# A product-key expert layer on one core: gates of the first half of the tokens are spread while the second half's top-k is still going on

## The chip, the cores and the metric

One core of a Trainium2 chip runs the whole program. The metric is the time of one execution in device microseconds (us); lower is better. All tensors are float32, and products of matrices are made from two parts of each operand (a high part rounded to a format that TensorE takes in one pass, and the low rest): three matmuls, high x high, high x low and low x high, stand for one.

## The reference, cut to what matters

The program is one layer block (modulation, attention, a recurrence, an expert layer) followed by a second one of two layers. The change lies in the expert layer, 256 tokens, width 1024, 16384 experts of one neuron each:

```python
def peer_ffn(h, w_query, sub_keys1, sub_keys2, expert_u, expert_v):
    q = (x @ w_query).reshape(T, 8, 256)
    s1 = einsum('thd,nd->thn', q[..., :128], sub_keys1)      # 128 keys
    s2 = einsum('thd,nd->thn', q[..., 128:], sub_keys2)
    v1, i1 = top_k(s1, 16)
    v2, i2 = top_k(s2, 16)
    cand = (v1[..., :, None] + v2[..., None, :]).reshape(T, 8, 256)
    top_s, top_p = top_k(cand, 16)
    e_idx = i1[top_p // 16] * 128 + i2[top_p % 16]
    gate = softmax(top_s, axis=-1)
    act = gelu(einsum('cd,ced->ce', x, expert_u[e_idx]))
    y = einsum('ce,ced->cd', gate * act, expert_v[e_idx])
```

## The kernel before, in words

The kernel gathers nothing. `peer` (L1026) goes over all 16384 experts in NB = 128 blocks of 128 (block j holds the experts whose first key is j). A first pass computes gelu(x u) for every expert and all 256 tokens and multiplies it by a gate that is 0 for the experts that a token did not choose; a second pass multiplies the result by v. The products of gate and gelu stay in SBUF: G0 holds blocks 0 to 71 (NA = 72), G1 blocks 72 to 127, each block 128 experts x 256 tokens.

*First pass.* `fetch` (L1180) loads one block of u as four transfers from SP's queue into a raw tile `u` (three buffers). `prepare(j)` (L1191) fetches block j+2, transposes block j on DVE (`uT`, three buffers), and makes its high part `uh` on ACT and its low part `ul` on POOL, two halves of 512 columns each (four buffers of either). `products(j)` (L1203) does 24 matmuls of 256 columns on PE, the gelu on ACT, then `prepare(j + 4)`, and then calls `advance`, which gives the side work its share of the block.

*Side work.* A list of generators is worked off by `advance` (L1248): a block brings `pace` units, each yield of a generator costs some. `topk` (L1089) is one head for one half (tile t of 128 tokens) of the tokens: two searches among 128 keys (1.2 units each), one among 256 candidates (1.4), and the lookup of the indices (1), nearly all on DVE; POOL does one multiplication of the lookup (`oh`), and DVE adds it up one step later (`looked_up`). `gates(t)` (L1120) makes the softmax of a half and transposes indices and gates into `pick`. `spread` (L1142) makes the dense gates, four tokens (N = 4) at a step: DVE writes two masks `one0` and `one1` by comparing a row of numbers with the indices, ACT scales `one1` by the gate (four activations), PE multiplies the two into a PSUM tile of 4 x 128 x 128, and this is brought into G: columns of blocks that are already finished are multiplied on DVE (`G<-G,g`), those that are not are copied by ACT (`G<-g`). The masks of a step are made one step ahead. A block that comes later than some gates multiplies its gelu by them in `products` (DVE, `G<-y,G`, where y is the gelu in PSUM). One spread tile takes one of four PSUM banks tagged g, as a block's product does.

Before the change the order of the side work is: the heads of tile 0, two heads of tile 1, `gates(0)`, the other heads of tile 1, `gates(1)`, and only then `spread` over all 256 tokens; its masks lie where the top-k tiles were. Pace is 1.3 during top-k and 1 after.

V, A and P are engines behind `Ordered` (L993), which keeps their instructions in the order in which the program writes them; they all show line L1001. In the trace L106 to L108 are the three matmuls of a product, L1162 the matmul of a spread step, L1312 to L1314 the second pass, L1188 the transfer of u.

The second pass (`second`, L1226) loads v into the raw tiles of `u` and `uT`, five blocks ahead, and makes its high and low parts in `uh` and `ul`.

Of the kernel before, what the change touches and what calls it, by code (L numbers as in the profile page):

```python
# [11 lines left out]
F = mybir.dt.float32  # L12
FR = mybir.dt.float32r
# [7 lines left out]
T = 256  # L21
# [1004 lines left out]
def peer(k, then):  # L1026


    nc, a, tc = k.nc, k.a, k.tc
    mod = k.mod  # L1030
    uu, vv = a["peer_u"][0], a["peer_v"][0]
    NB, NA = 128, 72
    V, A, P = (Ordered(tc, e) for e in (nc.vector, nc.scalar, nc.gpsimd))
    with ExitStack() as es:

# [15 lines left out]
        e2 = ExitStack()  # L1051
# [87 lines left out]
        state = dict(done=0, built=0)  # L1139
        N = 4  # L1140

        def spread(pool, first):  # L1142


            i128 = k.psum([128, 128], tag="o", bufs=2)
            V.tensor_copy(i128, i128s)

            def ones(t0):
                b, g = (pool.tile([128, N, 128], F, name=f"one{i}", bufs=2) for i in range(2))
                for o, i in ((b, 0), (g, 1)):  # L1150
                    V.tensor_tensor(o, i128[:, None, :].to_broadcast([128, N, 128]),
                                    pick[:, i, t0:t0 + N, None].to_broadcast([128, N, 128]), op=OP.is_equal)
                for t in range(N):
                    A.activation(g[:, t], g[:, t], AF.Copy, scale=pick[:, 2, t0 + t:t0 + t + 1])
                return b, g
            nxt = ones(0)
            yield 1
            for t0 in range(0, T, N):
                b, g = nxt
                p = k.psum([128, N, 128])  # L1160
                for t in range(N):
                    nc.tensor.matmul(p[:, t], g[:, t], b[:, t], start=True, stop=True)  # L1162
                if t0 + N < T:
                    nxt = ones(t0 + N)
                n = state["done"]
                for x, at in ((G[0], 0), (G[1], NA)):
                    x, y = x[:, :, t0:t0 + N], p.rearrange("p t j -> p j t")
                    to = at + x.shape[1]
                    c = min(max(n, at), to)
                    if c > at:  # L1170
                        V.tensor_tensor(x[:, :c - at], x[:, :c - at], y[:, at:c], op=OP.mult)
                    if c < to:
                        A.activation(x[:, c - at:], y[:, c:to], AF.Copy)
                state["built"] = t0 + N
                yield (NB - 5 - first) * N / T

        us = {}
        gap(k, pool, GAPS["u"])

        def fetch(j):  # L1180
            if j < NB:
                us[j] = pool.tile([128, 1024], F, name="u", bufs=3)
            elif j < 2 * NB:
                us[j] = pool.tile([128, 1024], F, name=("u", "uT")[j // 3 % 2], bufs=3)
                nc.sync.dma_start(us[j], vv[(j - NB) * 128:(j - NB) * 128 + 128])
            if j < NB:
                for x in range(4):
                    nc.sync.dma_start(us[j][32 * x:32 * x + 32].rearrange("p (g d) -> p g d", g=4),  # L1188
                                      uu[j * 128:j * 128 + 128, 256 * x:256 * x + 256].rearrange("(g p) d -> p g d", g=4))
# [12 lines left out]

        def products(j):  # L1203

            p = k.psum([128, T])
            h, l = (x.rearrange("p (c e) -> p c e", c=8) for x in us.pop(j))
            for c in range(8):
                k.mm3(p, h[:, c], l[:, c], ph[:, c], pl[:, c], c == 0, c == 7)
            n = state["built"]
            o = G[j // NA][:, j % NA]  # L1210
            if n:
                g = k.psum([128, T], tag="y", bufs=2)
                A.activation(g[:, :n], p[:, :n], AF.Gelu)
            if n < T:
                A.activation(o[:, n:], p[:, n:], AF.Gelu)
            if j + 4 < NB:
                prepare(j + 4)
            elif j + 4 == NB:
                for x in range(2, 5):
                    fetch(NB + x)  # L1220
            if n:
                V.tensor_mul(o[:, :n], g[:, :n], o[:, :n])
            state["done"] = j + 1
            advance(pace)

        def second(i):  # L1226

            r = us[NB + i]
            vh, vl = (pool.tile([128, 1024], FR, name=x, bufs=4) for x in ("uh", "ul"))
# [12 lines left out]
        best = [[], []]  # L1242
        side = []
# [27 lines left out]
        for _ in proj_t_steps(k, a["peer_w_query"][0], hh, hl, 0, 2048, use):  # L1271
            step += 1
            for x in best[0]:
                side.append(x)
            best[0].clear()
            advance(1.05)
            if 6 <= step < 22:
                for d, o in turns[:2]:
                    A.activation(d, o.bitcast(F), AF.Copy)
                del turns[:2]  # L1280
            elif step == 25:
                fetch(0)
                fetch(1)
# [837 lines left out]
```

## Time and profile before

| | us |
|---|---|
| three executions | 2318.8, 2332.5, 2334.44 (median 2332.5) |
| the profiled execution | 2320.28 |
| its span in the profile | 2318.2 |
| first pass over u in it | from 487.16 to 926.70 |

The profiled execution is near the fastest of the three. Rows of a timeline give the start, the duration, the engine, the line, the operation and the shape, xN for N instructions that follow each other, and in brackets how long the engine stood idle before and what released it. Instructions of one engine overlap by some hundredths of a microsecond, so the time from start to start is a little less than the duration.

### The profile page before, as it was taken

To read this page: it belongs to the slowest core of one execution; us is meant where nothing else is said; L and a number is where in the kernel's file an instruction comes from. 1 tells how busy PE (TensorE), PEld (TensorE's weight loads), DVE (VectorE), ACT (ScalarE), POOL (GpSimd) and SP (SyncE) were. 2 spreads that over 40 slices of the span, in tenths; PEclk is the share of its full clock that TensorE was granted. 3 is DMA by queue.
4 is the path that set the end of the run, shared out by engine and by line. 5 is a ranking of instruction groups with operands and counts; after the bars stand their busy time and mean duration, and the time that the engine had idled before them with its cause. 6 is when DMAs were issued, how large, how long until landed. Compare 5 with 4: busy or idle time off the path is not lost.

```text
span 2318.2 us, 46849 instructions
## 1 busy us (share of the span) xinstructions
PE 2191.8 (95%) x17962; PEld 2079.0 (90%) x17962; DVE 1735.9 (75%) x3278; ACT 1264.6 (55%) x2689; POOL 809.6 (35%) x811
## 2 busy tenths in 40 slices
PE   6999898789899999999999999899999999989998
PEld 3878587789799999999999999878899999979998
DVE  6888886899877888777776765678875666777664
ACT  3543532735477776555554644447556666536543
POOL 1132320569877777444444100101432221131000
PEclk8999898899999999999999999999999999989999
DMA  7422123447655666666665675323565555516663
GB/s 266 149 92 86 61 73 96 119 107 173 162 148 155 154 150 177 196 196 195 193 193 165 185 219 193 122 74 111 155 202 166 181 162 191 178 36 192 190 200 119
DMA packets 304064, 358.38 MB, mean 155 GB/s; under 512 B 24188, under 2 KB 276576, under 8 KB 302816
## 3 DMA queue, kind: packets, MB, share of 16 engines
q1 hardware_dynamic: 291456, 349.53, 50.0%
q10 hardware_dynamic: 12384, 5.86, 1.0%
q8 instruction: 141, 2.31, 0.4%
q14 instruction: 83, 0.68, 0.1%
HBM read 354.28 MB, written 1.05 MB: 153 GB/s over the span
## 4 chain that ended last, share of the span: by engine, by line
PE 76%; DVE 13%; DMA 3%; ACT 3%; issue 2%; POOL 2%; SPq 0%; ACTq 0%; DVEq 0%; POOLq 0%
PE g L106 12%; PE g L108 12%; PE g L107 12%; PE o L106 4%; PE o L107 4%; PE o L108 3%; PE g L1162 2%; PE y L1314 2%; PE o L1314 2%; PE y L1312 2%; PE o L1312 2%; PE o L1313 2%; PE y L1313 2%; DVE uT L1001 2%; DVE wl L100 2%
## 5 line engine op out<-in xcount | busy, mean ns | idle before, releaser
L99 ACT ACTIVATE wh<-raw 128x1024 fp32r<-128x1024 f32 (+3 forms) x397 | 387.1, 977 | 389.2 <-PE g L107 185.5
L100 DVE TENSOR_TENSOR wl<-raw,wh 128x1024 fp32r<-128x1024 f32 (+3 forms) x381 | 431.6, 1135 | 223.2 <-ACT wh L99 209.8
L106 PE MATMUL g<-xh,wh 128*128 128x256 f32 x1864 | 529.9, 285 | 8.7 <-ACT xh L374 5.8
L108 PE MATMUL g<-xh,wl 128*128 128x256 f32 x1864 | 525.4, 282 | 8.4 <-DVE wl L100 8.3
L107 PE MATMUL g<-xl,wh 128*128 128x256 f32 x1864 | 524.6, 282 | 4.1 <-DVE xl L375 2.7
L1001 POOL TENSOR_TENSOR ul<-uT,uh 128x512 fp32r<-128x512 f32 x320 | 411.6, 1306 | 188.4 <-ACT uh L1001 188.4
L106 PEld LDWEIGHTS g<-xh,wh 128*128 128x128 f32 x1864 | 357.5, 192 | 15.2 <-ACT xh L374 6.9
L108 PEld LDWEIGHTS g<-xh,wl 128*128 128x128 f32 x1864 | 356.2, 191 | 12.1 <-DVE wl L100 11.7
L107 PEld LDWEIGHTS g<-xl,wh 128*128 128x128 f32 x1864 | 356.4, 191 | 6.1 <-DVE xl L375 3.5
L1001 ACT ACTIVATE uh<-uT 128x512 fp32r<-128x512 f32 x384 | 221.3, 627 | 146.5 <-POOL ul L1001 76.5
L108 PE MATMUL g<-ph,ul 128*128 128x256 f32 x1024 | 291.1, 284 | 7.7 <-POOL ul L1001 7.6
L106 PE MATMUL g<-ph,uh 128*128 128x256 f32 x1024 | 292.8, 286 | 3.7 <-ACT uh L1001 2.0
L107 PE MATMUL g<-pl,uh 128*128 128x256 f32 x1024 | 289.1, 282 | 0.0
L108 PEld LDWEIGHTS g<-ph,ul 128*128 128x128 f32 x1024 | 194.7, 190 | 11.3 <-POOL ul L1001 11.1
L106 PE MATMUL o<-hh,wh 128*128 128x256 f32 x704 | 197.8, 281 | 1.6 <-DVE t L1374 1.6
L106 PEld LDWEIGHTS g<-ph,uh 128*128 128x128 f32 x1024 | 195.1, 191 | 4.6 <-ACT uh L1001 2.3
L107 PE MATMUL o<-hl,wh 128*128 128x256 f32 x704 | 197.4, 280 | 0.0
L108 PE MATMUL o<-hh,wl 128*128 128x256 f32 x704 | 197.1, 280 | 0.0
L107 PEld LDWEIGHTS g<-pl,uh 128*128 128x128 f32 x1024 | 195.3, 191 | 0.0
L1001 DVE TENSOR_TENSOR al<-G,ah 128x256 fp32r<-128x256 f32 x128 | 173.9, 1359 | 17.2
L154 POOL TENSOR_TENSOR sql<-sq,sqh 128x256 fp32r<-128x256 f32 x48 | 48.8, 1018 | 340.1 <-ACT sqh L153 336.0
L1001 DVE STREAM_TRANSPOSE uT<-u 128x1024 f32<-128x1024 f32 x128 | 157.8, 1235 | 2.3 <-DMA u<-in_peer_u_dram 1.9
(772 smaller groups left out, 5456.4 us busy)
## 6 DMA issues: line engine op xcount, KB each, us to landing
u<-in_peer_u_dram SPq DMA_DIRECT2D x512, 128.0 KB, 2.6
raw<-in_ffn_w_gate_dram SPq DMA_DIRECT2D x44, 1024.0 KB, 5.6
raw<-in_ffn_w_up_dram SPq DMA_DIRECT2D x44, 1024.0 KB, 5.3
u<-in_peer_v_dram SPq DMA_DIRECT2D x64, 512.0 KB, 4.3
uT<-in_peer_v_dram SPq DMA_DIRECT2D x64, 512.0 KB, 4.2
raw<-in_ffn_w_down_dram SPq DMA_DIRECT2D x32, 1024.0 KB, 5.1
raw<-in_ada_w_dram SPq DMA_DIRECT2D x24, 1024.0 KB, 5.2
raw<-in_w_in_dram SPq DMA_DIRECT2D x13, 1024.0 KB, 5.7
```

Of the source, the lines that this page charges most:

```text
L99: nc.scalar.activation(h, v, AF.Copy)
L100: self.sub.tensor_tensor(l, v, h.bitcast(F), op=OP.subtract)
L106: nc.tensor.matmul(out, sh, mh, start=first, stop=False)
L107: nc.tensor.matmul(out, sh, ml, start=False, stop=False)
L108: nc.tensor.matmul(out, sl, mh, start=False, stop=last)
L154: self.sub.tensor_tensor(l, sq, h.bitcast(F), op=OP.subtract)
L1001: return lambda *args, **kw: self.tc.keep_in_program_order(f(*args, **kw))
L1162: nc.tensor.matmul(p[:, t], g[:, t], b[:, t], start=True, stop=True)
L1312: nc.tensor.matmul(o, vh[:, s], ah, start=i == 0 and c % 2 == 0, stop=False, skip_group_check=True)
L1313: nc.tensor.matmul(o, vh[:, s], al, start=False, stop=False, skip_group_check=True)
L1314: nc.tensor.matmul(o, vl[:, s], ah, start=False, stop=i == NB - 1, skip_group_check=True)
```

## The change

Spreading the gates of tile 0 begins as soon as these exist, and runs between the pieces of tile 1's top-k (`both` takes from either generator in proportion 48 to 42 units); tile 1 is spread afterwards. So that tile 1's scores, which lie in G0, are not overwritten, blocks are worked in another order: 72 to 127 first (G1), then 0 to 71 (G0). The masks get tiles of their own beside the top-k tiles, and for that room the raw tile `u` has two buffers instead of three and `ul` three instead of four; u is fetched one block ahead, v four. Pace is 0.95, then 1.2 once `both` begins, then 1.

```diff
+    blocks = [*range(NA, NB), *range(NA)]
...
-        def spread(pool, first):
+        def spread(t, new, first=None):
...
             def ones(t0):
-                b, g = (pool.tile([128, N, 128], F, name=f"one{i}", bufs=2) for i in range(2))
+                b, g = (new(i, t0 // N % 2) for i in range(2))
...
-            nxt = ones(0)
-            yield 1
-            for t0 in range(0, T, N):
+            last = 128 * t + 128
+            nxt = ones(128 * t)
+            yield 1.5
+            for t0 in range(128 * t, last, N):
...
-                n = state["done"]
-                for x, at in ((G[0], 0), (G[1], NA)):
+                for x, at, n in ((G[0], 0, max(state["done"] - NB + NA, 0)), (G[1], NA, NA + state["done"])):
                     x, y = x[:, :, t0:t0 + N], p.rearrange("p t j -> p j t")
                     to = at + x.shape[1]
                     c = min(max(n, at), to)
                     if c > at:
                         V.tensor_tensor(x[:, :c - at], x[:, :c - at], y[:, at:c], op=OP.mult)
                     if c < to:
                         A.activation(x[:, c - at:], y[:, c:to], AF.Copy)
                 state["built"] = t0 + N
-                yield (NB - 5 - first) * N / T
+                yield 1.25 if first is None else (NB - 5 - first) * N / 128
...
-                us[j] = pool.tile([128, 1024], F, name="u", bufs=3)
+                us[j] = pool.tile([128, 1024], F, name="u", bufs=2)
...
-            fetch(j + 2)
+            fetch(j + 1)
             uT = pool.tile([128, 1024], F, name="uT", bufs=3)
-            h, l = (pool.tile([128, 1024], FR, name=x, bufs=4) for x in ("uh", "ul"))
+            h, l = (pool.tile([128, 1024], FR, name=x, bufs=n) for x, n in (("uh", 4), ("ul", 3)))
...
-            o = G[j // NA][:, j % NA]
+            o = G[blocks[j] // NA][:, blocks[j] % NA]
...
-            if i + 5 < NB:
-                fetch(NB + i + 5)
+            if i + 4 < NB:
+                fetch(NB + i + 4)
...
-        side += best[0] + best[1][:2] + [gates(0)] + best[1][2:] + [gates(1)]
+        ow = e2.enter_context(tc.tile_pool(reuse_waits="tile", name="po", bufs=1, side="right"))
+        new = lambda i, turn: ow.tile([128, N, 128], F, name=f"one{i}", bufs=2)
+        side += best[0] + [both(chain(gates(0), spread(0, new)), chain(*best[1], gates(1)), 48, 42)]
...
-        pace = 1.3
+        pace = 0.95
         for j in range(NB):
-            if not side and not state["built"]:
-                e2.close()
-                ow = e2.enter_context(tc.tile_pool(reuse_waits="tile", name="po", bufs=1, side="right"))
-                side.append(spread(ow, j))
+            if not side and state["built"] == 128:
+                assert blocks[j] < 46
+                side.append(spread(1, new, j))
                 pace = 1
```

In the built program PE's spread steps stand behind blocks 43 to 122 before, and behind 17 to 77 and 82 to 123 now.

DVE, one spread step late in the first pass of the kernel before, when G0 (G_4181) is finished and G1 (G_5114) in part; `one` are masks, `g` the spread tile, `y` a gelu in PSUM; what an instruction waits for stands in brackets:

```order
L1001 TENSOR_TENSOR G_5114<-y_10256,G_5114 128x180 [waits Activation_49]
L1001 TENSOR_TENSOR one_10278<-o_7192,pick 128x512 [waits DVE_49]
L1001 TENSOR_TENSOR one_10279<-o_7192,pick 128x512 [waits DVE_49]
L1001 TENSOR_TENSOR G_4181<-G_4181,g_10273 128x72x4 [waits PE_49]
L1001 TENSOR_TENSOR G_5114<-G_5114,g_10273 128x28x4 [waits Activation_49]
L1001 STREAM_TRANSPOSE uT<-u 128x1024 [waits DMAHW6_49,DMAHW1_49,DMAHW7_49,DMAHW0_49,Pool_49]
```

The first spread step with a finished block in the changed kernel, on DVE, where G1 is G_5109, with the pieces of top-k around it:

```order
L1001 MAX_INDEX ti<-tv,ks_5900 128x8 [waits DVE_49]
L1001 TENSOR_REDUCE nat_4233<-oh 128x2x16
L1001 STREAM_TRANSPOSE uT<-u 128x1024 [waits DMAHW4_49,DMAHW3_49,DMAHW5_49,DMAHW2_49,Pool_49]
L1001 TENSOR_TENSOR one_5951<-o_5851,pick 128x512
L1001 TENSOR_TENSOR one_5952<-o_5851,pick 128x512
L1001 TENSOR_TENSOR G_5109<-G_5109,g_5946 128x18x4 [waits Activation_49]
L1001 STREAM_TRANSPOSE uT<-u 128x1024 [waits DMAHW6_49,DMAHW1_49,DMAHW7_49,DMAHW0_49,Pool_49]
L1001 TENSOR_TENSOR G_5109<-y_5987,G_5109 128x4 [waits Activation_49]
L1001 TENSOR_TENSOR cand<-tv 128x256
```

The product on the spread tile g waited for PE, whose matmuls write it, and for ACT's gelu; now it waits for ACT alone.

ACT at a spread step of the kernel before:

```order
L1001 ACTIVATE one_10769<-one_10769,pick 128x128 [waits DVE_49,Activation_49]
L1001 ACTIVATE one_10769<-one_10769,pick 128x128 x3
L1001 ACTIVATE G_5114<-g_10763 128x19x4 [waits DVE_49,PE_49]
L1001 ACTIVATE y_10804<-g_10779 128x212 [waits PE_49]
L1001 ACTIVATE G_5114<-g_10779 128x44
```

ACT at the step of the changed kernel that was shown for DVE (same spread tile g_5946):

```order
L1001 ACTIVATE one_5952<-one_5952,pick 128x128 [waits DVE_49]
L1001 ACTIVATE one_5952<-one_5952,pick 128x128 x3
L1001 ACTIVATE G_4181<-g_5946 128x72x4 [waits PE_49]
L1001 ACTIVATE G_5109<-g_5946 128x38x4 [waits DVE_49]
L1001 ACTIVATE y_5987<-g_5962 128x4 [waits PE_49]
```

Before, ACT's one copy of the spread tile waited for DVE; now ACT's copy of G0 waits for PE, stands ahead of DVE's product, and ACT's copy of G1's rest waits for that product.

## Rows read from the trace of the kernel before

**Rows 1.** The page, busy time and instructions by engine.

```profile
PE 2191.8 (95%) x17962; PEld 2079.0 (90%) x17962; DVE 1735.9 (75%) x3278; ACT 1264.6 (55%) x2689; POOL 809.6 (35%) x811
```

**Rows 2.** Stretches: length, PE, PEld, DVE, ACT, POOL busy (instructions), clock, DMA share, GB/s.

```profile
483.50:634.50 151.00, 136.18 (x1098) 131.20 (x1097) 137.89 (x376) 73.38 (x147) 130.21 (x102) 0.98 0.68 160
487.16:560.00 72.84, 65.81 (x531) 63.39 (x530) 68.03 (x178) 35.65 (x71) 62.49 (x49) 0.98 0.69 159
560.00:620.00 60.00, 55.89 (x465) 54.05 (x464) 57.19 (x174) 27.60 (x57) 55.36 (x44) 1.00 0.68 167
...
645.00:926.70 281.70, 281.70 (x2484) 281.70 (x2483) 223.91 (x394) 215.58 (x660) 206.97 (x163) 1.00 0.60 157
926.70:1260.00 333.30, 333.30 (x2943) 333.30 (x2942) 251.92 (x247) 179.72 (x370) 158.18 (x124) 1.00 0.61 192
```

**Rows 3.** PE's timeline: first product of u, first of v.

```profile
487.16 0.36 PE L106 MATMUL g<-ph,uh 128*128 128x256 f32 x1
...
926.70 0.28 PE L1312 MATMUL o<-ah,uh 128*128 128x256 f32 x1
```

**Rows 4.** Groups by shape, 440 to 960 us: busy us, mean ns, idle before.

```profile
L106 PE MATMUL g<-ph,uh 128*128 128x256 f32 x1024 | 292.8, 286 | 3.7 <-ACT uh L1001 2.0 <-ACT G L1001 1.7
...
L1162 PE MATMUL g<-one,one 128*128 128x128 f32 x512 | 75.3, 276 | 2.8 <-ACT one L1001 2.8
...
L1001 DVE TENSOR_TENSOR G<-G,g 128x288 f32<-128x288 f32 x42 | 18.7, 444 | 0.1
...
L1001 ACT ACTIVATE uh<-uT 128x512 fp32r<-128x512 f32 x273 | 157.3, 629 | 77.2 <-DVE uT L1001 69.0 <-POOL ul L1001 8.2
...
L1001 ACT ACTIVATE G<-g 128x256 f32<-128x256 f32 x56 | 20.3, 371 | 6.6 <-PE g L1076 6.4
...
L1001 POOL TENSOR_TENSOR ul<-uT,uh 128x512 fp32r<-128x512 f32 x264 | 339.2, 1309 | 108.4 <-ACT uh L1001 108.4
```

**Rows 5.** DVE's groups, 483.5 to 634.5 us.

```profile
L1001 DVE STREAM_TRANSPOSE uT<-u 128x1024 f32<-128x1024 f32 x47 | 57.5, 1229 | 1.3 <-DMA u<-in_peer_u_dram 1.3
...
L1001 DVE TENSOR_REDUCE nat<-oh 128x32 f32<-128x512 bf16 x11 | 7.4, 670 | 5.9 <-POOL oh L1001 5.9
```

**Rows 6.** DVE's timeline at the start, at 702 and at 909 us.

```profile
494.99 3.49 DVE L1001 STREAM_TRANSPOSE uT<-u 128x1024 f32<-128x1024 f32 x3
...
537.41 0.69 DVE L1001 TENSOR_REDUCE nat<-oh 128x32 f32<-128x512 bf16 x1 [2.40 <-POOL oh L1001]
...
701.96 0.22 DVE L1001 TENSOR_TENSOR G<-y,G 128x56 f32<-128x56 f32 x1 [1.20 <-ACT y L1001]
702.10 1.28 DVE L1001 TENSOR_TENSOR one<-o,pick 128x512 f32<-128x512 f32 x2
...
909.16 0.42 DVE L1001 TENSOR_TENSOR G<-y,G 128x248 f32<-128x248 f32 x1 [1.15 <-ACT y L1001]
909.50 1.28 DVE L1001 TENSOR_TENSOR one<-o,pick 128x512 f32<-128x512 f32 x2
910.69 0.72 DVE L1001 TENSOR_TENSOR G<-G,g 128x288 f32<-128x288 f32 x2
911.33 1.24 DVE L1001 STREAM_TRANSPOSE uT<-u 128x1024 f32<-128x1024 f32 x1
912.79 0.42 DVE L1001 TENSOR_TENSOR G<-y,G 128x252 f32<-128x252 f32 x1 [0.23 <-ACT y L1001]
```

**Rows 7.** ACT's timeline of the step at 909 us.

```profile
910.87 1.28 ACT L1001 ACTIVATE one<-one,pick 128x128 f32<-128x128 f32 x4 [0.62 <-DVE one L1001]
912.06 0.16 ACT L1001 ACTIVATE G<-g 128x24 f32<-128x24 f32 x1
912.40 0.36 ACT L1001 ACTIVATE y<-g 128x252 f32<-128x252 f32 x1 [0.17 <-PE g L108]
```

**Rows 8.** Transfers of u: duration of the issue (ns), and to landing.

```profile
L1188 SPq DMA_DIRECT2D u<-in_peer_u_dram x512: 311/430/1808, 384.6 to 907.5; - x171
...
DMA to landing us min/median/max: 2.4/2.6/4.4
```

More of the change, by code (lines that the diff above doesn't have):

```diff
@@ L1162, in spread @@
                     nc.tensor.matmul(p[:, t], g[:, t], b[:, t], start=True, stop=True)
-                if t0 + N < T:
+                if t0 + N < last:
                     nxt = ones(t0 + N)
-                n = state["done"]
-                for x, at in ((G[0], 0), (G[1], NA)):
+                for x, at, n in ((G[0], 0, max(state["done"] - NB + NA, 0)), (G[1], NA, NA + state["done"])):
                     x, y = x[:, :, t0:t0 + N], p.rearrange("p t j -> p j t")
@@ L1181, in fetch @@
             if j < NB:
-                us[j] = pool.tile([128, 1024], F, name="u", bufs=3)
+                us[j] = pool.tile([128, 1024], F, name="u", bufs=2)
             elif j < 2 * NB:
-                us[j] = pool.tile([128, 1024], F, name=("u", "uT")[j // 3 % 2], bufs=3)
+                us[j] = pool.tile([128, 1024], F, name=("u", "uT")[j % 5 > 1], bufs=2 + (j % 5 > 1))
                 nc.sync.dma_start(us[j], vv[(j - NB) * 128:(j - NB) * 128 + 128])
             if j < NB:
+                j, u = blocks[j], us[j]
                 for x in range(4):
-                    nc.sync.dma_start(us[j][32 * x:32 * x + 32].rearrange("p (g d) -> p g d", g=4),
+                    nc.sync.dma_start(u[32 * x:32 * x + 32].rearrange("p (g d) -> p g d", g=4),
                                       uu[j * 128:j * 128 + 128, 256 * x:256 * x + 256].rearrange("(g p) d -> p g d", g=4))
         def prepare(j):
-            fetch(j + 2)
+            fetch(j + 1)
             uT = pool.tile([128, 1024], F, name="uT", bufs=3)
-            h, l = (pool.tile([128, 1024], FR, name=x, bufs=4) for x in ("uh", "ul"))
+            h, l = (pool.tile([128, 1024], FR, name=x, bufs=n) for x, n in (("uh", 4), ("ul", 3)))
             V.transpose(uT, us[j].rearrange("p (g b i) -> p b g i", g=4, b=8))
@@ L1218, in products @@
             elif j + 4 == NB:
-                for x in range(2, 5):
+                for x in range(1, 4):
                     fetch(NB + x)
@@ L1228, in second @@
             r = us[NB + i]
-            vh, vl = (pool.tile([128, 1024], FR, name=x, bufs=4) for x in ("uh", "ul"))
+            vh, vl = (pool.tile([128, 1024], FR, name=x, bufs=n) for x, n in (("uh", 4), ("ul", 3)))
             ah, al = (x[i % 4] for x in ahl)
@@ L1282, in peer @@
                 fetch(0)
-                fetch(1)
             elif step in (26, 29):
@@ L1288, in peer, with chain, both @@
         G.append(es.enter_context(tc.tile_pool(reuse_waits="tile", name="ph", bufs=1)).tile([128, NB - NA, T], F, name="G1"))
-        side += best[0] + best[1][:2] + [gates(0)] + best[1][2:] + [gates(1)]
+        def chain(*parts):
+            for x in parts:
+                yield from x
+        def both(x, y, sx, sy):
+            nonlocal pace
+            pace = 1.2
+            px = py = 0
+            while x or y:
+                if x and (not y or px * sy <= py * sx):
+                    cost = next(x, None)
+                    x, px = (None, px) if cost is None else (x, px + cost)
+                else:
+                    cost = next(y, None)
+                    y, py = (None, py) if cost is None else (y, py + cost)
+                if cost is not None:
+                    yield cost
+        ow = e2.enter_context(tc.tile_pool(reuse_waits="tile", name="po", bufs=1, side="right"))
+        new = lambda i, turn: ow.tile([128, N, 128], F, name=f"one{i}", bufs=2)
+        side += best[0] + [both(chain(gates(0), spread(0, new)), chain(*best[1], gates(1)), 48, 42)]
         prepare(2)
         prepare(3)
-        pace = 1.3
+        pace = 0.95
         for j in range(NB):
-            if not side and not state["built"]:
-                e2.close()
-                ow = e2.enter_context(tc.tile_pool(reuse_waits="tile", name="po", bufs=1, side="right"))
-                side.append(spread(ow, j))
+            if not side and state["built"] == 128:
+                assert blocks[j] < 46
+                side.append(spread(1, new, j))
                 pace = 1
```

## The prediction

> **What bounds the kernel now.** I read the page's busy line first [rows 1]: PE is busy for 95% of the span, so a change that leaves PE's work alone, as this one does, can give back no more than PE's holes. The table by stretch [rows 2] shows where the holes are in the expert stage: PE is full from 645 us on, and through the whole second pass (926.7 to 1260), but not between 487 and 645. The matmul timeline gives the edges of the first pass over the experts [rows 3]: its first product starts at 487.16, the second pass at 926.70, so it lasts 439.5 us. Its work is 3 x 1024 product matmuls and 512 for the gates [rows 4]; in the full second pass 2943 matmuls take 333.3 us [rows 2], 0.1133 us each, so 3584 of them need 405.9 us. The pass loses 33.6 us. From 560 to 620 DVE is busy 57.2 of 60 us while PE issues 465 matmuls where a full PE would issue 530 [rows 2]: DVE is the limit there. From 483.5 to 634.5 it is busy 137.9 us [rows 2], 57.5 of it in transposes, one per block [rows 5] and 1.16 us from start to start (three in 3.49 [rows 6]); the rest is top-k.
>
> In the second part of the pass it is the other way round. One spread step there reads [rows 6, 7]: DVE multiplies a finished block by its gates (909.16), makes two masks (909.50), multiplies finished columns of both gate tiles (910.69), transposes (911.33), and is then idle 0.23 us until ACT has the next gelu. In that step DVE waits for ACT only at the gelu, which is PE's pace. ACT scales the second mask from 910.87, 0.09 us after DVE ended, and copies the columns that are not finished at 912.06, behind the four scalings.
>
> **The change part by part.** *PE.* The same 3584 matmuls; the 64 spread steps of four tokens stand behind blocks 17 to 123 instead of 43 to 122. Cost 0, if the rest keeps up. What is to be had is the 33.6 us, less what the start keeps: from 487.16 to 560 PE issues 531 matmuls, worth 60.1 of 72.8 us [rows 2], and there the order on DVE is nearly the old one. So the aim is about 405.9 + 12.7, or 21 us less than now.
>
> *The order of G1 and G0.* Before, finished columns lie in G0 until block 72, so of a spread tile DVE multiplies its part first and ACT copies the rest after it. Now the first 56 blocks are G1's, but the loop still takes G0 first: ACT copies all of G0, and only then may DVE multiply G1's finished part. The order of the changed kernel shows it: the product on G1 waits for ACT alone, no longer for PE, in all 64 steps (from block 56 on, G0's finished part, ACT's copy of G0's rest, G1's part). ACT's copy stands behind the four scalings, and these wait for the masks that DVE has made just before. So DVE must stand still for a chain that did not bind it: masks 1.28 us [rows 6], 0.09 to ACT, four scalings 1.19 from the first to the copy [rows 7], the copy, 0.03 back (912.76 to 912.79 [rows 6, 7]). From the masks' start this is 2.59 us plus the copy. Before, the products started 1.19 us after the masks (909.50 to 910.69).
>
> Priced by step: in 20 steps (behind blocks 17 to 54) the copy is 288 columns wide, 0.40 us (0.371 at 256 [rows 4], 0.16 at 24 [rows 7]), and the product on G1 takes 0.22 from start to start: 2.59 + 0.40 + 0.22 = 3.21 us. In 12 steps (56 to 77) copy 0.36, product 0.30: 3.25. In the 32 steps of the second tile of tokens (82 to 123) copy 0.24, product 0.30: 3.13. Together 64.2 + 39.0 + 100.2 = 203.4 us. Unwaited they were 1.41 (1.19 + 0.22) in the first group and 1.83 (1.19 + 0.64 for two products [rows 6]) in the others, together 108.7; the wait adds 94.7 us to DVE. Queued behind the waiting product are the next transpose, the next block's product and all top-k pieces, and behind the transpose ACT's high part, POOL's low part and PE's block four later.
>
> The trace shows that DVE's products and ACT's copy on one spread tile do not overlap: 910.69 to 911.41 and 912.06 to 912.22 [rows 6, 7]. The Trainium skill's page "PSUM — Partial Sum Buffer", section "PSUM bank collisions raise a hardware error", says that two engines must not touch one bank in the same partitions at the same time, two readers included, so that the program has to put them in order. By that rule the new order has to be paid as a wait; if both might read at once, the sum would be that of the first rival.
>
> *DVE's whole chain.* From 483.6, when its first transpose begins:
> - 128 transposes x 1.16 = 148.5.
> - Top-k and gates: the same ten heads and two gates as before in 483.5 to 634.5. At least 137.9 - 57.5 = 80.4 [rows 2, 5]; at most all that is neither a transpose (48 x 1.16 = 55.7) nor a listed wait (5.9 + 1.3 [rows 5]) of 151, 88.1. I take 84, in the middle, as neither end has the better row.
> - Products of finished blocks, 0.14 us at 56 columns (701.96 to 702.10 [rows 6]) and 0.33 at 248 (909.16 to 909.50 [rows 6]): 64 at 66 columns on average, 0.15, and 45 at 192, 0.28, together 22. There are 25 more of them than before, since spreading begins earlier: some 4 of the 22.
> - Steps 203.4, and the first masks of either half 3.
> - Waits at the start, 12 (below).
>
> The sum is 473 us, so DVE ends at 957. The last block's transpose stands some 5 us before that end, and PE's block starts about 3.5 us behind it (1.24, then ACT's half of 0.63 and POOL's of 1.31 [rows 4], and the hand-overs) and takes 2.7, so the pass ends near 959.5 instead of 926.7: 32.8 us later. The same sum for the kernel before (84 wide products 18, steps 64 x 1.64 = 105) is 359 us, under PE's 405.9: it was DVE's crowding in the first third that cost, not its total. Now its total is the limit: per block it needs about 3.7 us, PE 3.2.
>
> *One raw tile of u less.* A tile is now fetched when the transpose two blocks earlier ends. Four issues of 0.43 us and a landing of 2.6 us behind the last [rows 8] are about 4.3 us. At 3.7 us a block there are 2 x 3.7 - 1.2 = 6.2 us, so it is hidden, but not where transposes stand together: three times at the start (the run of three 2 to 4, and two pairs in the order), 3 + 1.5 + 1.5 = 6 us. To this comes the wait for POOL's lookup before the gates, 2.4 us as before [rows 6], and about 4 us in blocks 78 to 81, where DVE has little to do and PE sets the pace: 12 us. If every landing took 4.4 us, as the slowest in this pass [rows 8], two blocks would need 1.2 + 1.7 + 4.4 = 7.3 us, 3.65 a block, against 3.7: then every light block waits.
>
> *One low part of u less.* POOL may begin block j+4 when PE has ended block j+1, so it has two blocks (over 6 us) for 2.6 us: hidden, at 0, and at worst part of the third rival. In the second pass the same rule leaves two blocks, 5.4 us, for 0.7 us on DVE and 1.3 on POOL: 0. Its prefetch of four tiles instead of five still leaves over 9 us for one transfer: 0.
>
> So the pass gains the 33.6 us of holes it has, and gets back 66 us of new ones. Against the profiled execution (span 2318.2, 2320.28 in all) that is 2353 us. Four executions are known: 2318.8 and 2320.28, 2332.5 and 2334.44. I set the difference on the middle between the two pairs, 2326.5, and get 2359 us; 1%, about what a measurement can tell from no change, is 23 us.
>
> **Rivals.** *The wait does not bind.* If ACT had the copy ready before DVE asks, DVE's sum would be 473 - 94.7 = 378 us, under PE's 405.9, and the pass would end 21 us earlier: 2305. For it speaks that DVE idles at every step today; against it that the idle time is 0.23 us in the late steps and the chain behind the masks over 1.2. This case is not slower; 0.9% faster by itself, over 1% only if the start also loses less.
>
> *Half of it binds.* In the second half PE has 3.63 us per step block (909.16 to 912.79 [rows 6]) and DVE would need 1.16 + 0.28 + 3.13 = 4.57, but in the ten blocks without a step only 1.46 against 2.72. If PE's lead in those blocks absorbs most of the 32 x 1.3 = 41.6 us, DVE's chain ends at about 920 and the time is 2320. Against it: PE can run ahead by only two or three blocks, as each holds one of four product banks, and 32 x 0.94 is more than 10 x 1.26.
>
> *The raw tiles bind too.* With landings of 4.4 us the 64 blocks without a step have DVE stand 0.4 us each on average, 25 us on top: 2384. For it: 16 engines are at 0.6 share already [rows 2]; against it: median 2.6.
>
> **How the numbers follow.** Forecast 0.62, no binding wait 0.10, half 0.15, raw tiles too 0.13. The forecast's own spread is 12 us either way (top-k 4, waits 6, the width of copies and the tail the rest). Slower by over 1% are the raw tiles' case and nearly all of the forecast: 0.71. Within 1% are the half case, half of the first rival and a rest of the forecast: 0.24. Faster 0.05. The range reaches from the half case to the raw tiles' case: 2318 to 2388.
>
> **What would show it.** DVE's idle time before the products on G (G<-G,g, 0.1 us for 42 of them today [rows 4]) must become about 1.4 us each, 64 to 100 times, released by ACT's copy of G. PE's busy share in 560 to 900 must fall below nine tenths, with its waits on POOL's low part; the first spread matmul must come near 545 us, and the second pass must start near 960. It is wrong if the products on G wait for nothing or PE is full from 560 on; if DVE's transposes wait long on the transfers of u, the third rival holds.

## The result, and the profile after

The changed kernel takes 2391.6 us in the median of four executions (2384.75 to 2406.82) against 2331.7 for the kernel before: ratio 1.0285, 95% interval 1.0257 to 1.0312. It is slower, as forecast, but by 60 us, where a time of 2359 us had been said, and it lies 3.6 us outside the range. The ratios here and below are estimates with an interval, not quotients of the medians shown. The profiled execution took 2384.75 us, with a span of 2383.0 (before 2318.2).

The page's busy line and the shares of the chain that ended last, of the changed kernel, answer to [rows 1]:

```profile
PE 2225.2 (93%) x17962; PEld 2101.7 (88%) x17962; DVE 1745.2 (73%) x3308; ACT 1273.8 (53%) x2713; POOL 874.3 (37%) x811
...
PE 63%; DVE 19%; ACT 6%; issue 5%; DMA 4%; POOL 3%; SPq 1%; DVEq 0%; ACTq 0%; POOLq 0%
```

PE issues the same 17962 matmuls. Its share of the chain was 76% before, and DVE's 13%. Three stretches of the changed kernel answer to [rows 2] (length, then busy time and instructions of PE, weight loads, DVE, ACT, POOL, then granted clock, DMA share, GB/s): the whole first pass, its part from 640 us on, and 300 us of the second pass.

```profile
489.08:985.19 496.11, 444.78 (x3597) 432.04 (x3596) 365.21 (x801) 302.70 (x845) 342.34 (x269) 0.98 0.54 141
640.00:985.19 345.19, 311.29 (x2538) 303.38 (x2537) 249.10 (x512) 216.47 (x627) 230.58 (x181) 0.98 0.53 139
985.19:1285.19 300.00, 300.00 (x2647) 299.89 (x2646) 234.29 (x223) 161.27 (x332) 199.44 (x111) 1.00 0.60 194
```

The first pass lasts 496.1 us instead of 439.5: 56.6 of the 64.8 us between the two spans. Where PE was full before, from 640 us on, it is now idle for a tenth. The second pass is as full as it was. DVE's waits in the pass (who waits, for whom, us in total, times, longest):

```profile
DVE G L1001 <- ACT G L1001: 92.0, 64, 1.7
DVE uT L1001 <- DMA u<-in_peer_u_dram: 13.6, 13, 2.0
DVE G L1001 <- ACT y L1001: 6.8, 4, 2.8
DVE uT L1001 <- POOL ul L1001: 5.0, 2, 3.5
DVE uT L1001 <- POOL oh L1001: 4.4, 2, 2.5
```

and PE's waits from 480 to 990 us:

```profile
PE g L1165 <- ACT one L1001: 38.8, 36, 4.9
PE g L108 <- POOL ul L1001: 5.5, 9, 0.9
PE g L106 <- ACT G L1001: 4.4, 11, 0.7
```

The first line of DVE's is the new wait: in all 64 steps the product on G waits for ACT's copy of G. One such step on DVE's timeline (start, us, engine, operation):

```profile
704.38 1.27 DVE L1001 TENSOR_TENSOR one<-o,pick 128x512 f32<-128x512 f32 x2
707.35 0.38 DVE L1001 TENSOR_TENSOR G<-G,g 128x220 f32<-128x220 f32 x1 [1.70 <-ACT G L1001]
```

and on ACT's:

```profile
705.74 1.28 ACT L1001 ACTIVATE one<-one,pick 128x128 f32<-128x128 f32 x4 [0.23 <-DVE one L1001]
706.93 0.39 ACT L1001 ACTIVATE G<-g 128x288 f32<-128x288 f32 x1
```

Masks, four scalings, the copy of all 288 columns of G0 (706.93 to 707.32), and 0.03 us later DVE's product: 2.97 us from the masks' start, where the prediction's chain gives 2.59 + 0.40. PE, in turn, waits for the masks, which DVE makes late because it stood still one step earlier; with that wait taken away (the first experiment) PE's waits for masks fall from 38.8 us to 12.6.

### The profile page after: what moved, and what is told of

It is laid out like the page before. It is cut to its first block, busy times and chain, and to the rows that moved or that the text cites. A ratio compares the mean times of both kernels' runs of the same rounds, so it can differ in the third digit from the quotient of the medians.

```text
span 2383.0 us, 47110 instructions
## 1 busy us (share of the span) xinstructions
PE 2225.2 (93%) x17962; PEld 2101.7 (88%) x17962; DVE 1745.2 (73%) x3308; ACT 1273.8 (53%) x2713; POOL 874.3 (37%) x811
## 4 chain that ended last, share of the span: by engine, by line
PE 63%; DVE 19%; ACT 6%; issue 5%; DMA 4%; POOL 3%; SPq 1%; DVEq 0%; ACTq 0%; POOLq 0%
PE g L106 9%; PE g L108 9%; PE g L107 8%; DVE uT L1001 4%; PE o L106 3%; PE o L107 3%; PE o L108 3%; ACT one L1001 3%; DVE one L1001 2%; DMA u<-in_peer_u_dram 2%; PE o L1336 2%; PE o L1334 2%; PE y L1334 2%; PE y L1336 2%; PE o L1335 2%
## 5 line engine op out<-in xcount | busy, mean ns | idle before, releaser
L1001 POOL TENSOR_TENSOR ul<-uT,uh 128x512 fp32r<-128x512 f32 x333 | 466.4, 1418 | 224.7 <-ACT uh L1001 75.8
L106 PEld LDWEIGHTS g<-xh,wh 128*128 128x128 f32 x1864 | 358.5, 193 | 15.6 <-ACT xh L374 6.7
L1001 ACT ACTIVATE uh<-uT 128x512 fp32r<-128x512 f32 x410 | 236.4, 624 | 252.2 <-DVE uT L1001 157.5
L108 PEld LDWEIGHTS g<-xh,wl 128*128 128x128 f32 x1864 | 357.6, 192 | 11.1 <-DVE wl L100 10.7
L1001 DVE TENSOR_TENSOR al<-G,ah 128x256 fp32r<-128x256 f32 x128 | 194.1, 1516 | 0.0
L1001 DVE STREAM_TRANSPOSE uT<-u 128x1024 f32<-128x1024 f32 x128 | 158.3, 1237 | 23.9 <-DMA u<-in_peer_u_dram 13.6
L154 POOL TENSOR_TENSOR sql<-sq,sqh 128x256 fp32r<-128x256 f32 x48 | 49.2, 1029 | 337.5 <-ACT sqh L153 336.0
```

Source lines behind the costliest of these rows:

```text
L106: nc.tensor.matmul(out, sh, mh, start=first, stop=False)
L108: nc.tensor.matmul(out, sl, mh, start=False, stop=last)
L154: self.sub.tensor_tensor(l, sq, h.bitcast(F), op=OP.subtract)
L1001: return lambda *args, **kw: self.tc.keep_in_program_order(f(*args, **kw))
```

## The experiments

None of them leaves out any work; ratios are against runs of the kernel before beside them. In the table, "first pass" is the stretch from the first product of u to the first of v in the profiled execution, and "after" counts the matmuls of the 40 us that begin 337.5 us behind that, when the second pass is nearly over (left out for the two kernels whose second pass was longer, below). Both are read from one profile each. Two kernels have a second profile: their first passes are 441.0 and 441.8 us, and 439.6 and 434.7 us. A difference of less than some 5 us between two first passes is therefore not told apart from chance.

| kernel | median us | ratio to before (95%) | first pass us | after |
|---|---|---|---|---|
| before | 2331.7 | | 439.5 | 294 |
| changed | 2391.6 | 1.0285 (1.0257 to 1.0312) | 496.1 | 262 |
| changed, G1 first | 2348.0 | 1.0089 (1.0059 to 1.0119) | 446.0 | 261 |
| before, both tiles fewer | 2352.7 | 1.0124 (1.0077 to 1.0171) | 455.2 | 264 |
| before, G1 first | 2362.9 | 1.0143 (1.0123 to 1.0162) | 476.5 | 292 |
| before, one low part less | 2341.5 | 1.0039 (1.0018 to 1.0059) | 441.0 | |
| before, one raw tile less | 2343.4 | 1.0050 (1.0027 to 1.0072) | 453.7 | 294 |
| G1 first, small masks, 3 raw | 2382.0 | 1.0219 (1.0186 to 1.0251) | 480.1 | 262 |
| G1 first, small masks, 4 low | 2388.1 | 1.0249 (1.0215 to 1.0282) | 490.7 | 293 |
| G1 first, 3 raw, 2 transposed | 2335.1 | 1.0037 (1.0011 to 1.0064) | 439.6 | |
| changed, 3 raw, 2 transposed | 2384.1 | 1.0233 (1.0201 to 1.0266) | 485.3 | 264 |

The theory at the start: the order of G0 and G1 makes the wait, and the wait makes the loss. The rival: the tiles that were given up make it.

**The changed kernel with G1 first.** The step works the finished tile first, as the kernel before did in its first half:

```diff
-for x, at, n in ((G[0], 0, max(state["done"] - NB + NA, 0)), (G[1], NA, NA + state["done"])):
+for x, at, n in ((G[1], NA, NA + state["done"]), (G[0], 0, max(state["done"] - NB + NA, 0))):
```

> The changed kernel with one edit: the loop over the gate tiles takes G1 first and G0 second, so DVE's product on finished columns stands ahead of ACT's copies again. Theory (the order of G0 and G1 makes the cost): DVE's waits on ACT's copy of G, 92.0 us in 64 in the changed kernel, fall under 10 us, and the first pass from 496 us to between 419 and 435 us, as PE's 406 us of matmuls and the start are then the limit; time 2315 to 2330 us, 0.99 to 1.00 of the kernel before. Rival A (the missing raw tile and low part make the cost): over 2370 us, DVE still waiting on transfers and POOL. Rival B (top-k and spreading side by side make it, by short stops of PE that lower its clock): near 2350 us, with PE's granted clock still under 0.95 in several stretches of 20 us.

2348.0 us, and the first pass is 446.0 us long. DVE's waits in it:

```profile
DVE G L1001 <- ACT y L1001: 35.1, 64, 2.3
DVE uT L1001 <- DMA u<-in_peer_u_dram: 16.7, 19, 2.5
DVE uT L1001 <- POOL ul L1001: 10.9, 9, 3.5
```

The wait on the copy is gone from the list; DVE waits for the gelu again, which is PE's pace. So the order costs 50.1 us of the pass. But 18 us against the kernel before remain, and waits of the transposes for transfers of u and for POOL stand where [rows 5] had 1.3 us. (Of the 17.4 us between the two profiled spans 6.4 lie in the first pass and 10.0 behind the second pass, a part that is 1044 to 1055 us long in the four kernels with four low parts; what makes it vary so stays open.)

Rival B had the time, near 2350, but not the reason. Of the stretches of 20 us from 480 us on, four have a granted clock of 0.91; in the kernel before three have 0.95 or less (one of them 0.88). The kernel with two transposed tiles, below, spreads as early, and in its second profile it has one such stretch and a first pass of 434.7 us. In the changed kernel there are six, down to 0.83; they come with PE's waits, and no run parts their cost from that of the waits.

**The kernel before with both tiles fewer.** Only the edits of the buffers and of the prefetch, none of the order:

```diff
-us[j] = pool.tile([128, 1024], F, name="u", bufs=3)
+us[j] = pool.tile([128, 1024], F, name="u", bufs=2)
-fetch(j + 2)
+fetch(j + 1)
...
-h, l = (pool.tile([128, 1024], FR, name=x, bufs=4) for x in ("uh", "ul"))
+h, l = (pool.tile([128, 1024], FR, name=x, bufs=n) for x, n in (("uh", 4), ("ul", 3)))
```

> The kernel before with the changed kernel's buffers alone: two raw tiles of u, three low parts, u fetched one block ahead and v four. Theory (the order of G0 and G1): these cost at most the 6 to 12 us of waits at the start, 2331 to 2344 us, ratio 1.000 to 1.005. Rival A: most of the 60 us, over 2360 us.

It takes 23 us more than the kernel before, not 0 to 12: the theory's price for the tiles was too low. Its first pass is 15.6 us longer.

**The kernel before with the wait alone.** Its loop over the two gate tiles is turned round:

```diff
-for x, at in ((G[0], 0), (G[1], NA)):
+for x, at in ((G[1], NA), (G[0], 0)):
```

> The kernel before with the wait alone: the loop over the gate tiles takes G1 first, which here (G0 is finished first) puts an ACT copy ahead of DVE's product in every spread step. Theory: DVE waits some 1.4 us in each of 64 steps, 90 us, of which its idle time in the second part of the pass (about 56 us) covers a part: 25 to 45 us longer, 2357 to 2377 us. Rivals A and B: nothing of theirs is in it, so no more than 5 us longer.

33 us, inside what was expected; the first pass is 37 us longer. The wait, by itself, in a kernel that has all its tiles and spreads late (DVE's waits):

```profile
DVE G L1001 <- ACT G L1001: 94.7, 64, 1.7
```

Theory and rival are both right, then, for different parts. The next two runs part the tiles.

**One low part less**, alone in the kernel before (of the edit above the line of `h, l`, in both passes):

> The kernel before with three low parts of u and v in place of four, raw tiles and order of the work untouched. Theory (each of the two missing tiles costs about half of the 23 us that both cost together): 2336 to 2346 us; in the first pass POOL's low part waits for PE (70 to 80 us in all, off the path), PE waits for POOL's low part 12 to 18 us (7.6 before), DVE's transpose for POOL's low part 5 to 8 us (none before), and for the transfer of u no more than 3 us; and after the second pass the next stage is about 4 us late, 260 to 270 matmuls in its first 40 us against 296. Rival (the raw tile alone costs): within 3 us of the kernel before, 2327 to 2333. Rival (the low part alone costs): 2348 to 2356.

**One raw tile less**, alone in the kernel before (the other lines of that edit):

> The kernel before with two raw tiles of u in the first pass and the transfer of one block ahead in place of three and two, low parts and order of the work untouched. Theory: 2336 to 2346 us; DVE's transpose waits 10 to 14 us for transfers of u (1.9 before), most of it in the first sixteen blocks, no wait of the transpose for POOL's low part, and the stage after the second pass starts as in the kernel before. Rival (the low part alone costs): 2327 to 2333. Rival (the raw tile alone costs): 2348 to 2356.

Both totals fit "about half each", but the places differ. The first pass without the low part is 441.0 us, 1.4 more than before, which is not clear of chance; without the raw tile it is 453.7, 14.1 more. DVE's waits there, raw tile missing:

```profile
DVE G L1001 <- ACT y L1001: 51.4, 77, 2.3
DVE uT L1001 <- DMA u<-in_peer_u_dram: 12.9, 14, 1.7
...
DVE uT L1001 <- POOL ul L1001: 5.6, 3, 3.5
DVE uT L1001 <- POOL oh L1001: 5.4, 5, 1.4
```

The transposes wait 23.9 us, against 1.9 in the kernel before: 12.9 for transfers, as expected, though all of it behind block 16 and none before, and 11.0 for POOL, at its low parts and lookups, where I had expected none. That these come with the raw tile the run shows, but not how. Without the low part the transposes wait 1.9 us for transfers and 1.1 us, once, for POOL's low part, where 5 to 8 were expected, and PE waits 8.9 us for POOL's low part, not 12 to 18: that part of the expectation was wrong. The low part's price lies elsewhere, behind the second pass. These are 40 us of the kernel before and of the changed one, from the same place (337.5 us behind the first product of v):

```profile
1264.20:1304.20 40.00, 36.66 (x294) 36.09 (x293) 26.30 (x39) 24.61 (x46) 10.43 (x17) 0.91 0.58 180
```

```profile
1322.69:1362.69 40.00, 34.43 (x262) 32.88 (x261) 26.46 (x36) 23.08 (x44) 12.78 (x18) 0.87 0.47 141
```

32 matmuls, 3.6 us at 0.1133 us each. In the table the count is 261 to 264 wherever there are three low parts (255 in the second profile of the kernel with two transposed tiles, which is not in the table) and 292 to 294 wherever there are four. DVE's last low part and last product of the pass, before and after:

```profile
1264.78 0.69 DVE L1001 TENSOR_TENSOR ul<-uT,uh 128x512 fp32r<-128x512 f32 x1 [0.53 <-ACT uh L1001]
1265.61 1.37 DVE L1001 TENSOR_TENSOR al<-G,ah 128x256 fp32r<-128x256 f32 x1
```

```profile
1325.84 0.69 DVE L1001 TENSOR_TENSOR ul<-u,uh 128x512 fp32r<-128x512 f32 x1 [0.59 <-issue]
1326.45 1.51 DVE L1001 TENSOR_TENSOR al<-G,ah 128x256 fp32r<-128x256 f32 x1
```

and POOL's last two low parts, before and after:

```profile
1262.68 1.29 POOL L1001 TENSOR_TENSOR ul<-u,uh 128x512 fp32r<-128x512 f32 x1 [1.43 <-ACT uh L1001]
1265.40 1.29 POOL L1001 TENSOR_TENSOR ul<-uT,uh 128x512 fp32r<-128x512 f32 x1 [1.43 <-ACT uh L1001]
```

```profile
1323.15 1.81 POOL L1001 TENSOR_TENSOR ul<-uT,uh 128x512 fp32r<-128x512 f32 x1 [0.90 <-PE y L1336]
1325.87 1.81 POOL L1001 TENSOR_TENSOR ul<-u,uh 128x512 fp32r<-128x512 f32 x1 [0.91 <-POOL ul L1001]
```

With four low parts these wait for ACT's high part. With three, the last but one, like nearly all in that pass, waits for PE to free a buffer; for the last the trace names POOL itself. DVE's last product ends at 1266.98 before, 2.8 us behind the mark of 1264.20, and at 1327.96 after, 5.3 us behind 1322.69. The next stage's weights land in the room of that pool; their loads are issued 0.02 and 0.03 us behind that end, and ACT splits the first at 1272.53 and at 1333.69, 8.3 and 11.0 us behind the mark.

**Small masks, and a tile given back.** Masks of two tokens instead of four for the first tile of tokens (`N=2`, 64 steps of half the size), in the kernel with G1 first; the room goes to the raw tile in one run and to the low part in the other. The second tile of tokens keeps masks of four, which lie where the top-k tiles were, as in the kernel before.

```diff
-def spread(t, new, first=None):
+def spread(t, new, first=None, N=4):
...
-side += best[0] + [both(chain(gates(0), spread(0, new)), chain(*best[1], gates(1)), 48, 42)]
+side += best[0] + [both(chain(gates(0), spread(0, new, N=2)), chain(*best[1], gates(1)), 48, 42)]
```

> The changed kernel with G1 worked before G0 in the spread step and the third raw tile given back; its room comes from masks of two tokens instead of four while the first tile of tokens is spread (64 steps of half the size in place of 32; the second tile is spread with four as before). Theory: the tile takes back about half of the 18 us by which the kernel with the order swapped was longer than the kernel before, and the smaller steps give some of it back, DVE being the limit there: 2335 to 2350 us. If small steps cost nothing: 2325 to 2338. If they cost as much as large ones each (32 more steps of about 1.3 us of masks on DVE): 2360 to 2385.

> As the run with masks of two tokens and the third raw tile, but the room goes to the fourth low part and the raw tiles stay at two. Theory: 2335 to 2350 us as well, with the stage after the second pass back to 290 to 300 matmuls in its first 40 us and DVE's transpose waiting for transfers of u 13 to 17 us. If the low part costs nothing it is 8 to 12 us longer than the run with the third raw tile; if the raw tile costs nothing, as much shorter.

2382.0 and 2388.1: both far above what theory said, and the first is what the case of full price for each step gave. The reason is not the one I wrote there. DVE's mask of two tokens takes 0.410 us where one of four takes 0.677, some 9 us more over the 32 doubled steps; most of the rest are PE's waits for masks, 42.0 us in 21 times, where the kernel with G1 first and full masks has 12.6 in 7. The masks are made one step ahead, which is half as much time now; that a top-k piece on DVE uses it up fits the waits, but no run parts it. The granted clock of that stretch is below 1.00 (before, [rows 2], it was 0.98 to 1.00):

```profile
549.00:800.00 251.00, 214.66 (x1707) 210.83 (x1708) 194.89 (x535) 146.42 (x469) 163.25 (x129) 0.94 0.52 128
```

Between themselves the two runs say the same as the pair above: the third raw tile is worth 10.6 us of the first pass, the fourth low part 31 matmuls behind the second. In the run with four low parts the transposes wait 9.3 us for transfers, not 13 to 17.

**The raw tile given back out of the transposed tiles**, two of these in place of three; once with G1 first, once in the changed kernel as it is:

```diff
-us[j] = pool.tile([128, 1024], F, name="u", bufs=2)
+us[j] = pool.tile([128, 1024], F, name="u", bufs=3)
-fetch(j + 1)
-uT = pool.tile([128, 1024], F, name="uT", bufs=3)
+fetch(j + 2)
+uT = pool.tile([128, 1024], F, name="uT", bufs=2)
```

> The changed kernel with G1 worked before G0 and the third raw tile given back; its room comes from the transposed tiles, two in place of three, and not from the masks. Theory (the raw tile carries the loss of the first pass, the low part only a few us after the second): the transpose's waits for transfers of u fall from 16.7 us to 2 to 4, the first pass from 446 us to 432 to 440, and the total to 2326 to 2340 us, level with the kernel before or a little under it. Rival (two transposed tiles hold DVE up at POOL's low part as much as the raw tile did at the transfers): the transpose waits 12 us or more for POOL, the pass stays at 444 to 450 and the total at 2343 to 2353.

> The changed kernel itself, G0 still before G1, with the third raw tile given back out of the transposed tiles, as in the run beside it. Theory (the two costs add up): the first pass falls from 496 us by 10 to 16, the total to 2373 to 2383 us; DVE's waits of its product on G1 for ACT's copy of G0 stay at 88 to 98 us in 64 steps. Rival (the wait on G0's copy hides the late transfers, so that only the larger of the two is paid): 2386 to 2395.

With G1 first the total is 2335.1 us, the first pass 439.6: nothing is left of the loss there, though the transposes still wait 12.0 us for transfers, where 2 to 4 were expected, and 23.2 for POOL, which is the rival's wait (12 or more) without the rival's time. So the theory's total came out and its reason only in part: what carries these waits in this kernel no run shows. It is still 0.4% over the kernel before, not under it. In the changed kernel the pass falls by 10.9 us, as expected, the total to 2384.1, 1 us over the theory's range and 2 under the rival's. DVE's waits there:

```profile
DVE G L1001 <- ACT G L1001: 92.4, 64, 2.0
DVE uT L1001 <- POOL ul L1001: 13.6, 10, 2.2
DVE G L1001 <- ACT y L1001: 5.4, 4, 2.3
...
DVE uT L1001 <- DMA u<-in_peer_u_dram: 1.4, 2, 1.2
```

The wait on the copy is what it was, the transfers' is gone (1.4 us), though 13.6 us for POOL have come: in the first pass the two costs add, and neither hides the other. The total alone, between the two ranges, would not have told.

**Two kernels a second time.** In the profiles of one low part less and of G1 first with three raw tiles, the second pass itself was some 14 us longer than in the others, at a full granted clock.

> The kernel before with three low parts once more, for a second profile. In its first one the matmuls of the second pass stood 0.118 us apart at a granted clock of 1.00 (254 in 30 us, 267 in the kernel before), which made that pass 13.5 us longer. Theory (the distance is drawn anew in each execution and is no cost of the low part): in an execution of 2330 to 2337 us the second pass has 0.1133 us, and what is left of the low part's cost is 3 to 5 us after that pass. Rival (three low parts slow the second pass): 0.118 us again whatever the total is.

> The kernel with G1 first, three raw tiles and two transposed ones once more, for a second profile; twelve executions lay at 2327 to 2341 us (nine) and at 2352 to 2357 (three), and the profiled one of 2352 had 0.118 us from matmul to matmul in the second pass. Theory: at 2327 to 2341 us the second pass has 0.1133 us, at 2352 to 2357 it has 0.118. Rival (the tiles slow the second pass): 0.118 in both.

150 us from 1000 us on, in the second pass: G1 first with three raw tiles in its first profile (2352.4 us) and in its second (2334.8 us).

```profile
1000.00:1150.00 150.00, 150.00 (x1276) 150.00 (x1275) 112.66 (x106) 77.45 (x159) 95.21 (x53) 1.00 0.58 187
```

```profile
1000.00:1150.00 150.00, 150.00 (x1326) 150.00 (x1325) 116.74 (x111) 80.35 (x165) 98.74 (x55) 1.00 0.60 194
```

1276 matmuls or 1326, 0.1176 or 0.1131 us each: one kernel has both, so there the tiles don't set it. The kernel with one low part less had 1276 both times (2343.7 and 2339.2 us). Its second profile is not from the 2330 to 2337 us for which theory had spoken, so theory is not settled there. The longer distance stands in three of nine profiles with three low parts and in none of four with four. Whether three low parts make it likelier stays open; of the 0.4%, some 9 us, by which this kernel is over the kernel before, 1.4 are in the first pass, some 3.6 behind the second, and the rest are not attributed.

## Why the prediction was right or wrong

*The direction and the mechanism: right.* DVE's product on G1 stands behind ACT's copy of G0 in all 64 steps; 94.7 us were said and 92.0 measured, longest 1.7. Taking the order away took 50.1 us off the first pass, putting it into the kernel before added 37.0. The path from there to PE was another than forecast: of PE's 51.3 idle us in the pass 38.8 are waits for masks and 5.5 for POOL's low part, which was to be the wait.

*DVE's work: right.* The chain without its waits was 473 - 94.7 - 12 = 366 us; DVE is busy 365.2 us in the pass. PE's cost of 0 and the second pass itself held too.

*The step that failed: "Waits at the start, 12", and in it "it is hidden, but not where transposes stand together: three times at the start".* The size at the start came out, in part by luck: up to 540 us the transposes wait 5.5 us for transfers, against 6, but at blocks 11 to 15; the run of blocks 2 to 4, which had 3 of the 6, waits for no transfer. 8.1 us more come later in the pass, where two blocks were to cover 4.3 us, and transposes stood 5.0 us behind POOL's low parts and 4.4 behind its lookups, of which only 2.4 had been said. With 6.8 for the gelu and 1.4 for PE these waits make 31 us, 19 more than the 12. The pass ended 25.7 us later than 959.5: beside the 19 the first transpose is 3 us late (486.6 against 483.6), the new wait takes 2.7 off, and some 6 are left. Of these 3.6 lie in the tail: the second pass starts 11.1 us behind the last transpose's start (974.1), where 7.5 (from 952 to 959.5) had been taken, and the prediction's own terms for it, 3.5 and 2.7, make only 6.2. The prediction took an average of 3.7 us a block for cover, and the blocks are not alike. At the start top-k pieces put transposes close together in some and far apart in others. Of the 8.1 us later, 1.4 stand at block 49, with top-k beside it, 2.9 at blocks 83 to 86, transposed between the two tiles of tokens, where hardly a step is made, and 3.8 at blocks 98 to 124, where of the two stretches between three transposes one holds no spread step and is short. In all 13 cases 4.5 to 6.0 us passed between the end of the transpose two blocks earlier and the start of the one that waited, not 4.3.

*One low part less: 0 was said, for the first pass and the second.* In the first it is 1.4 us (2.3 in a second profile), not clear of chance, in the second nothing that is shown, but the stage behind waits for its last buffer: 3.6 us. I looked for who waits inside the pass, not for who needs the pool's room when it closes.

*The aim, "21 us less than now" if nothing else binds: too high.* The first pass goes in three steps: tiles given up +15.6 (439.5 to 455.2), early spreading with G1 first -9.2 (to 446.0), G0 first +50.1 (to 496.1). So the early spreading, which the change is made of, gives back 9 us in these profiles, and the tiles that pay for its masks cost more than that. The medians of the two kernels, 2352.7 and 2348.0, differ by only 4.7 us, and their intervals overlap, so the gain itself is not shown beyond chance. The run with G1 first is the rival "the wait does not bind" made true: it takes 2348.0 us, 43 more than the 2305 of that rival.

*The other rivals.* "Half of it binds" fell: of the 56.6 us, 29 are there when block 82 begins, and 27 come after that. "The raw tiles bind too" was nearest in size (2384), with 25 us from light blocks and landings of 4.4 us; what was measured for the raw tile is 10.9 to 14.1 us of the pass. Light blocks are where part of the waits stand, but the landings are not longer: 2.6 us in the median and 3.9 at most. *What would show it*: the first spread product came at 554.9, not near 545, the second pass at 985, not 960; PE's busy share in 560 to 900 is 0.897, just under nine tenths as said.

From 2359 to 2391.6: 24 us in the first pass, 3.6 behind the second, and 5 because the kernel before lies at 2331.7 and not at 2326.5. That these meet the total is partly luck: in the two profiles the part behind the second pass differs by 6.0 us, and these profiles lie 64.8 us apart, not 60.

## What to carry to other kernels

A loop over two tiles has an order, and when the work that meets it is renumbered, the order that was free becomes a wait: here one swapped line is worth 44 of 60 us. Buffers taken from a prefetch are not paid by the mean time per block but where transposes bunch, and the stage that reuses the pool's room pays for the last of them. When two changes stand in one edit, a run of the old kernel with each alone gives the prices: those of the two tiles agree with adding up (1.4 + 14.1 us of the first pass against 15.6, each from one profile), that of the wait depends on what stands beside it (37 us in the old kernel, 50 in the new).

## What was not expected of the hardware

Matmuls of one shape, with no wait, at a granted clock of 1.00, follow each other every 0.113 or every 0.118 us, over hundreds of microseconds, in one and the same kernel. For the 3072 matmuls of the second pass that is 347 or 361 us. What chooses between them no run here shows.

POOL's low part of 512 columns takes 1.81 us in the changed kernel's second pass and 1.29 before; the medians are 1.81 or 1.82 in all nine profiles with three low parts and 1.29 in all four with four. In the changed kernel it starts within 0.03 us of DVE's low part (0.69 us); before, it starts 0.6 us behind it. DVE's product behind it goes from 1.37 to 1.52 us. The Trainium skill's page "SBUF — State Buffer", section "Who interferes with whom", says that a VectorE instruction with two inputs in SBUF and a GpSimd instruction that reads SBUF exclude each other, and that the loser stands still. The trace agrees, nearly in size too: the 0.52 us by which POOL is longer are somewhat less than the 0.66 for which DVE's part still runs when POOL starts. In both kernels DVE's product of 256 columns takes twice as long as its low part of 512 and ends 0.28 us behind POOL's part.

After a wait of PE the granted clock can fall for a while. In the changed kernel PE waits 4.1 us for a mask before 809.5. This is the stretch of 20 us around it, and two pieces of it behind the wait:

```profile
800.00:820.00 20.00, 15.88 (x114) 15.68 (x114) 11.33 (x19) 9.52 (x28) 10.67 (x9) 0.83 0.55 137
809.50:812.00 2.50, 2.50 (x12) 2.50 (x13) 0.95 (x3) 2.11 (x8) 0.00 (x0) 0.50 0.74 137
816.00:820.00 4.00, 4.00 (x38) 4.00 (x37) 2.11 (x4) 2.44 (x8) 3.40 (x3) 1.00 0.46 112
```

Right behind the wait the clock is at 0.50, the lower of its two levels (1.2 and 2.4 GHz), with 12 matmuls in 2.5 us; from 816 us on it is full again, with 38 in 4 us. The 20 us have 114 matmuls where the 20 us behind them have 173; some 36 of the difference are the wait itself (4.1 us at 0.113), the rest come with the clock.
